# Weight loads on ScalarE's queue, paired transfers, a fourth slot and narrower tracking of overlaid tiles in a two-layer streaming encoder

## The chip, the cores and the metric

The kernel runs on the 8 cores of one Trainium2 chip (two dies of four cores). Each core works on its own stretch of a prompt and one running stream. The time is device microseconds of the slowest core, the median of several executions. Some executions fall in a slower state, in which the cores of one die or of both show a lower granted clock; they are marked slow and only fast runs are compared. PE is the matmul engine, DVE is VectorE, ACT is ScalarE, POOL is GpSimd, SP is SyncE, which here only issues transfers. PSUM is the memory, in eight banks, that matmuls write; an *evacuation* is the instruction that empties a bank.

## The reference, cut to what matters

```python
def trunk_layer(x, ...):
    xn = rms_norm(x, norm_mix)
    q, k, v, pin, gates = split(xn @ w_in)
    a  = sliding_window_attention(rms_norm(q), rms_norm(k), v, sinks)   # window 128
    pl = pool_mixer(pin)                 # trailing means over 2/4/8/16, minus the token
    g  = sigmoid(gates + gate_bias)
    x  = x + (g[0] * (a @ w_br_attn) + g[1] * (pl @ w_br_pool)) @ w_out # the mixer
    h  = causal_conv3(rms_norm(x, norm_ffn) @ w_up)
    return x + (gelu(h_gate) * h_value) @ w_down                        # the ConvFFN
# two layers; 1024 channels, 5632 up-projected channels; prompt frames and a few sampled frames
```

## The kernel before

A core works in phases: mixer of layer 1, ConvFFN of layer 1, mixer and ConvFFN of layer 2. A phase goes group by group, some 512 frames each. In a mixer group I call the gates and branch products with the next group's attention in between *stage E*, the output projection with its residual *F*, and the next projections *B*. The weights of mixer and ConvFFN do not fit together, so the tiles of one phase lie over those of the other. A small scheduler in the kernel records all operations and derives the waits. This is how it treated overlaid tiles:

```python
def op(self, eng, fn, reads=(), writes=()):
    w = list(writes)
    for r in writes:
        for x in self.over.get(r, ()):      # tiles of the other phase on the same bytes
            if x not in w:
                w.append(x)                 # counted as written too
    o.reads = tuple(reads); o.writes = tuple(w)
# _analyze: each write waits for the last writer and the readers of each name in o.writes
```

Weights and x go through SP's queue, and x tiles (`xsl`) through three rotating slots. A slot that is filled in two pieces gets the second piece only when the first has landed:

```python
def load_w(l, n):
    ...
    dma(wt[n][:, 0:sz], wb[i, :, 0:sz], [f"wb{i}"], wres(n), st)          # SP by default

def xload(src, src_res, pair, segs, zero=None):
    i = xst["n"] % NXS                                                    # NXS = 3
    for (a, b, t) in segs:
        dma(xs[i][:, :, a:b], ..., [f"xs{i}"], f"xs{i}")
```

At a change from mixer to ConvFFN ("hand-over") 17 weight tiles are loaded, the last nine after the output projection has been recorded:

```python
if nxt is None:
    load_w(l, "up6"); load_w(l, "up7")
...
stage_F(l, g)                       # issues the residual x loads
if nxt is None:
    for n in ("up8", "up9", "up10", "dn0", "dn1", "dn2", "dn3", "dn4", "dn5"):
        load_w(l, n)
```

Of the kernel before, what the change touches and what calls it, by code (L numbers as in the profile page):

```python
# [6 lines left out]
F32 = mybir.dt.float32  # L7
# [17 lines left out]
NXS = 3  # L25
NWS = 12
NFG = 9


class _Op:  # L30
    __slots__ = ("eng", "fn", "reads", "writes", "kind", "stream", "is_output", "eidx", "sidx",
                 "waits", "signal", "sig", "K", "epoch", "gidx")


class Sched:
# [24 lines left out]
    def op(self, eng, fn, reads=(), writes=()):  # L60
        o = _Op()
        w = list(writes)
        for r in writes:
            for x in self.over.get(r, ()):
                if x not in w:
                    w.append(x)
        o.eng = eng; o.fn = fn; o.reads = tuple(reads); o.writes = tuple(w)
        o.kind = "op"; o.stream = None; o.is_output = False
        o.waits = []; o.signal = False; o.sig = None; o.K = None; o.epoch = self.epoch
        o.gidx = len(self.ops)  # L70
        self.ops.append(o)
        return o

    def dma(self, eng, fn, reads=(), writes=(), stream=None, is_output=False):
        o = self.op(eng, fn, reads, writes)
        o.kind = "dma"
        o.stream = stream
        o.is_output = is_output
        if stream not in self.stream_sem:
            self.stream_sem[stream] = self.es.enter_context(self.nc.semaphore(f"dsem_{stream}"))  # L80
            self.stream_cnt[stream] = 0
        o.sidx = self.stream_cnt[stream]
        self.stream_cnt[stream] += 1
        if is_output:
            self.out_streams.add(stream)
        return o

    def _analyze(self):
# [5 lines left out]
        for op in self.ops:  # L94
# [9 lines left out]
            for wr in op.writes:  # L104
# [3 lines left out]
                for rd in readers.get(wr, ()):  # L108
                    if rd is not op and rd not in deps:
                        deps[rd] = "war"  # L110
            if op.kind == "dma":
# [3 lines left out]
                stream_last[op.stream] = op  # L115
            for r in op.reads:
# [120 lines left out]
def build_nc():  # L237
# [41 lines left out]
    with es:  # L279
# [23 lines left out]
        expAB = [sb("expA_s", [128, 8, 128], F32), sb("expB_s", [128, 8, 128], F32)]  # L303
# [4 lines left out]
        wpt = [sb(f"wpt_s{l}", [128, 512], BF16) for l in range(2)]  # L308
        kcache = [sb(f"kcache{l}", [128, 128], BF16) for l in range(2)]
        Vcache = [sb(f"Vcache{l}", [128, 2, 66], BF16) for l in range(2)]  # L310
        sph = [sb(f"sph_s{l}", [128, 4, 16], F32) for l in range(2)]
        hists = [sb(f"hists{l}", [128, NCH, 2], F32) for l in range(2)]
        Vg0 = sb("Vg0", [128, 3, 2, 66], BF16)
        Vsam = sb("Vsam", [128, 2, 66], BF16)
# [30 lines left out]
        ug = [su("f", f"ug{i}", [128, 512], F32) for i in range(3)]  # L345
        uv = [su("f", f"uv{i}", [128, 512], F32) for i in range(3)]
        for n, sz in FFN_UNITS[11:]:
            wt[n] = su("f", "w_" + n, [128, sz], BF16)

        xn1 = su("m", "xn1", [128, KT, 512], BF16)  # L350
        xn = [xn0, xn1]
        qT = su("m", "qT", [128, 4, 512], BF16, [(f"qT{j}", j * 1024, (j + 1) * 1024) for j in range(4)])
        kT = [su("m", f"kT{i}", [128, 512], BF16) for i in range(2)]
        Vw = [su("m", f"Vw{i}", [128, 4, 2, 66], BF16, [(f"Vw{i}_{t}", t * 264, (t + 1) * 264) for t in range(4)])
              for i in range(2)]
        pinb = [su("m", f"pinb{i}", [128, 528], F32) for i in range(2)]
        win = [su("m", f"win{i}", [128, 528], F32) for i in range(2)]
        dT = [su("m", f"dT{i}", [128, 4, 512], BF16, [(f"dT{i}_{j}", j * 1024, (j + 1) * 1024) for j in range(4)])
              for i in range(2)]
        P32 = [su("m", f"P32_{i}", [128, 1024], F32) for i in range(2)]  # L360
        PT = [su("m", f"PT{i}", [128, 2, 1024], BF16, [(f"PT{i}_{x}", x * 2048, (x + 1) * 2048) for x in range(2)])
              for i in range(2)]
# [3 lines left out]
        aT = [su("m", f"aT{i}", [128, 4, 512], BF16) for i in range(2)]  # L366
        tg = [[su("m", f"tg{a}{i}", [128, 512], F32) for i in range(2)] for a in range(2)]
        mixT = su("m", "mixT", [128, KT, 512], BF16, [(f"mixT{m}", m * 1024, (m + 1) * 1024) for m in range(KT)])
        sq = [su("m", f"sq{i}", [128, 512], BF16) for i in range(2)]
        srt = [su("m", f"srt{i}", [128, 512], F32) for i in range(2)]  # L370

        kg0 = su("m", "kg0", [128, HALO + TS], BF16)
        o32 = su("m", "o32", [128, 128], F32)
        kn32s = su("m", "kn32s", [128, TS], F32)
        pss = su("m", "pss", [128, 4, 16], F32)
        phist = su("m", "phist", [128, 4, 16], F32, [(f"ph{j}", j * 64, (j + 1) * 64) for j in range(4)])

        xnS = su("m", "xnS", [128, KT, 18], BF16)
        aTS = su("m", "aTS", [128, 4, 18], BF16)
        dTS = su("m", "dTS", [128, 4, 18], BF16, [(f"dTS{j}", j * 36, (j + 1) * 36) for j in range(4)])  # L380
        mixS = su("m", "mixS", [128, KT, 18], BF16, [(f"mixS{m}", m * 36, (m + 1) * 36) for m in range(KT)])

        def over(name, base, n):
            off = base[1]
            t = nc.alloc_sbuf_tensor_at(name, [128, KT, n], F32, offset=off)
            for p in range(4):
                S.region(f"{name}{p}", off + p * 8 * n, off + (p + 1) * 8 * n, "s")
            return t
        xst0 = over("xst0_", offs["P32_0"], HALO + TS)
        xst1 = over("xst1_", offs["aT0"], 512)  # L390

        actT = su("f", "actT", [128, NJ, 512], BF16, [(f"actT{j}", j * 1024, (j + 1) * 1024) for j in range(NJ)])

        corr = su("f", "corr", [128, NCH, 2], F32)
        ctmp = su("f", "ctmp", [128, NCH], F32)

        hso = su("f", "hso", [128, NCH, 2], F32)

        hpo = su("f", "hpo", [128, NCH, 2], F32)
# [28 lines left out]
        def dma(out, in_, reads, writes, stream, is_output=False, eng="sp"):  # L428
            S.dma(eng, lambda e: e.dma_start(out=out, in_=in_), reads=reads, writes=writes, stream=stream, is_output=is_output)
# [7 lines left out]
        def load_first(n):  # L437
# [4 lines left out]
            dma(wt[n][:, 0:sz], wun[i, :, 0:sz], [], wres(n), st, eng="pool")  # L442

        def load_w(l, n):
            i = l * NU + UIDX[n]
            sz = UNITS[UIDX[n]][1]
            st = f"w{wseq['n'] % NWS}"
            wseq["n"] += 1
            dma(wt[n][:, 0:sz], wb[i, :, 0:sz], [f"wb{i}"], wres(n), st)
# [13 lines left out]
        def xload(src, src_res, pair, segs, zero=None):  # L463
            i = xst["n"] % NXS
            xst["n"] += 1
            for (a, b, t) in segs:
                dma(xs[i][:, :, a:b], src[2 * pair:2 * pair + 2, :, t:t + b - a].rearrange("k p t -> p k t"),
                    src_res(pair, t, b - a), [f"xs{i}"], f"xs{i}")
# [19 lines left out]
        class NormJob:  # L488
# [12 lines left out]
            def load(self, p):  # L501
                if self.keep is not None:
                    t, nm = self.keep
                    for (a, b, c) in self.segs:
                        dma(t[:, 2 * p:2 * p + 2, a:b], self.src[2 * p:2 * p + 2, :, c:c + b - a].rearrange("k p t -> p k t"),
                            [], [f"{nm}{p}"], f"{nm}{p}")
# [46 lines left out]
            def scales(self):  # L553
                for p in range(3):
                    self.load(p)
                for p in range(3):
                    self.scale(p)
                self.load(3)
                self.scale(3)

            def stats(self):
                for p in range(4):
                    self.load(p)
                    self.stat(p)
                self.stat_end()
# [5 lines left out]
        def homes(g):  # L571
            b = g.par
            g.off = 0
            g.eX = (xn[b], f"xn{b}")
# [5 lines left out]
        def mixer_groups(l):  # L580
# [22 lines left out]
            g.att.append(dict(col=pe, n=TS, q0=0, nkc=TS, kp=(kcache[l][:, :], f"kcache{l}"), vp=(Vcache[l][:, :, :], f"Vcache{l}"),  # L603
# [5 lines left out]
            else:  # L609
                g.off = g.C0  # L610
# [45 lines left out]
        def qk_job(l, G, w, wr, c, a, gain_off, dests):  # L656
            bk = PB.get()
            X, xr = xn[G.par], f"xn{G.par}"
# [11 lines left out]

        def stage_B(l, G, fill=()):

            X, xr = xn[G.par], f"xn{G.par}"
# [15 lines left out]
            def pool_in(j):  # L689
# [3 lines left out]
                r = j % 2  # L693
                if G.own:
                    copy("pool", pinb[r][:, 0:16], phist[:, j, :], [f"ph{j}"], [f"pinb{r}"])
                    act(pinb[r][:, 16:528], psb[:, bk, 0:512], ACTF.Copy, pr(bk), [f"pinb{r}"])
                    n = 512
                else:
                    n = G.PE - G.C0
                    act(pinb[r][:, 0:16 + n], psb[:, bk, P0:G.PE], ACTF.Copy, pr(bk), [f"pinb{r}"])  # L700
                window(G, j, r, n, G.C0)
                copy("pool", phist[:, j, :], pinb[r][:, n:n + 16], [f"pinb{r}"], [f"ph{j}"])
                if G.samp is not None:
                    copy("pool", pinb[r][:, 0:16], sph[l][:, j, :], [f"sph{l}"], [f"pinb{r}"])
                    act(pinb[r][:, 16:16 + TS], psb[:, bk, G.samp:G.samp + TS], ACTF.Copy, pr(bk), [f"pinb{r}"])
                    window(G, j, r, TS, G.samp)
                    copy("pool", pss[:, j, :], pinb[r][:, 16:32], [f"pinb{r}"], ["pss"])
# [19 lines left out]
            for vi, (c, n, dst, rn, t) in enumerate(vt):  # L727
                bk = PB.get()
                for k in range(KT):
                    mm(psb[0:n, bk, 0:128], X[:, k, c:c + n], wkv[:, k, 128:256], k == 0, k == KT - 1, ["w_kv", xr], pr(bk))  # L730
                src = psb[0:n, bk, 0:128]
                copy("dve", dst, src.rearrange("p (g d) -> p g d", g=2), pr(bk), [rn])
                if t is None:
# [651 lines left out]
```

## Time and profile before

The time before is 3829.57 us (median of 3 runs; one of them, 4084.1 us, was slow; a fourth took 3828.24). I cut the profiled execution (slowest core, 3836.7 us) where the matmul stream changes its stage:

| stage, up to the first matmul named | us | PE busy |
|---|---|---|
| start, to stage E of group 1 | 259.4 | 111.5 |
| mixer 1, to stage E of the last group | 603.8 | 559.2 |
| first hand-over, to the second group's up-projection | 271.6 | 178.5 |
| ConvFFN 1, to the small group's keys in layer 2 | 882.7 | 861.4 |
| change of layer, to stage E of group 1 | 124.1 | 70.7 |
| the next group | 118.8 | 94.6 |
| mixer 2 | 513.0 | 476.7 |
| second hand-over | 239.5 | 172.9 |
| ConvFFN 2 | 823.9 | 820.1 |

Length minus PE busy is the time in which the matmul engine stood still, 491 us in all. The prediction shows these views with slightly other cuts in the hand-overs and at the change of layer.

### The profile page before, as it was taken

Reading aid. Unit: us, or ns where it says so; the run is one execution under the profiler, and the core shown is the slowest. Engines: PE = TensorE matmul, PEld = TensorE weight load, DVE = VectorE, ACT = ScalarE, POOL = GpSimd, SP = SyncE. Lnnn points to the kernel's source line nnn. Section 1 sums busy time; section 2 is a strip of 40 time slices with the busy share of each in tenths; the row PEclk is TensorE's granted clock in tenths of the full one; section 3 lists DMA queues with packets and bytes.
Section 4 is the critical chain, followed back from the end, with each engine's and each line's share of the span. In section 5 each row is a group of like instructions: output and inputs, shape, how many; then the busy total and the mean of one; then the engine's idle time right before and its main releaser. Section 6 shows DMA issues by size and latency. Waiting matters only on the chain.

```text
span 3836.7 us, 54933 instructions; the slowest of 8 cores (3823.3 to 3836.7 us)
## 1 busy us (share of the span) xinstructions
PE 3345.6 (87%) x17810; PEld 1621.7 (42%) x17810; DVE 2135.0 (56%) x3383; ACT 1545.1 (40%) x2432; POOL 1186.7 (31%) x1084
## 2 busy tenths in 40 slices
PE   1579999996599999999975879999966999999999
PEld 0344444442244444444432434444423455555554
DVE  1345455542376776666643444555426766666666
ACT  1244444431234555444433434433314444444444
POOL 1234443321123333322234333333213222333322
PEclk9789999998799999999987989999988999999999
DMA  6326666446623333333353223233252222222221
GB/s 128 69 74 132 127 130 128 122 109 165 185 79 103 92 85 90 95 98 101 106 170 92 50 82 97 88 94 104 76 192 91 81 73 80 80 79 79 79 64 40
DMA packets 186666, 384.37 MB, mean 100 GB/s; under 512 B 32880, under 2 KB 112400, under 8 KB 178384
## 3 DMA queue, kind: packets, MB, share of 16 engines
q1 hardware_dynamic: 181088, 324.00, 28.0%
q0 software_dynamic: 5296, 56.86, 9.6%
q8 instruction: 147, 2.41, 0.3%
q14 instruction: 135, 1.11, 0.1%
HBM read 368.09 MB, written 115.41 MB: 126 GB/s over the span
## 4 chain that ended last, share of the span: by engine, by line
PE 62%; DMA 17%; DVE 6%; POOL 5%; ACT 4%; issue 4%; SPq 1%; DVEq 0%; ACTq 0%; POOLq 0%
PE psb L413 61%; DMA xsl_67<-xT 3%; POOL win_114 L419 1%; DMA xsl_67<-xm 1%; POOL win_115 L419 1%; DMA xsl_66<-xT 1%; DMA xst__146<-xT 1%; DMA xsl_67<-x 1%; POOL PT_121 L419 1%; DMA xst__147<-xT 1%; DMA xsl_66<-x 1%; DMA xsl_66<-xm 1%; DMA xsl_68<-x 1%; ACT P_0_118 L416 1%; DVE xn_71 L422 1%
## 5 line engine op out<-in xcount | busy, mean ns | idle before, releaser
L419 POOL TENSOR_TENSOR actT<-ug_94,uv_97 128x480 bf16<-128x480 f32 (+3 forms) x126 | 148.7, 1180 | 1057.1 <-ACT ug_94 L416 939.6
L416 ACT ACTIVATE ug_94<-psb,pv 128x480 f32<-128x480 f32 (+3 forms) x144 | 106.4, 739 | 698.2 <-PE psb L413 520.5
L422 DVE SCALAR_TENSOR_TENSOR ug_94<-psb,pv,ug_94 128x480 f32<-128x480 f32 (+3 forms) x288 | 202.7, 704 | 137.5 <-ACT hso L416 73.5
L422 DVE SCALAR_TENSOR_TENSOR uv_97<-psb,pv,uv_97 128x480 f32<-128x480 f32 (+3 forms) x288 | 202.3, 702 | 17.2 <-issue 0.6
L422 DVE SCALAR_TENSOR_TENSOR ug_96<-psb,pv,ug_96 128x480 f32<-128x480 f32 (+3 forms) x252 | 177.6, 705 | 52.4 <-ACT ug_96 L416 27.9
L422 DVE SCALAR_TENSOR_TENSOR ug_95<-psb,pv,ug_95 128x480 f32<-128x480 f32 (+3 forms) x252 | 177.4, 704 | 22.8 <-ACT ug_95 L416 6.7
L419 POOL TENSOR_TENSOR actT<-ug_95,uv_98 128x480 bf16<-128x480 f32 (+3 forms) x126 | 148.7, 1180 | 128.9 <-ACT ug_95 L416 116.4
L422 DVE SCALAR_TENSOR_TENSOR uv_99<-psb,pv,uv_99 128x480 f32<-128x480 f32 (+3 forms) x252 | 177.0, 702 | 14.7 <-DVE uv_99 L422 0.9
L422 DVE SCALAR_TENSOR_TENSOR uv_98<-psb,pv,uv_98 128x480 f32<-128x480 f32 (+3 forms) x252 | 177.3, 704 | 14.0 <-DVE uv_98 L422 0.5
L419 POOL TENSOR_TENSOR actT<-ug_96,uv_99 128x480 bf16<-128x480 f32 (+3 forms) x108 | 127.4, 1179 | 159.3 <-ACT ug_96 L416 120.8
L413 PE MATMUL psb<-xn_71,w_up_83 128*128 128x482 bf16 (+3 forms) x576 | 122.4, 373 | 55.3 <-DVE xsl_68 L422 55.3
L419 POOL TENSOR_TENSOR win_114<-pinb_113 128x526 f32<-128x526 f32 (+7 forms) x40 | 37.1, 928 | 412.0 <-ACT pinb_113 L416 411.7
L419 POOL TENSOR_TENSOR PT_121<-P_0_118,expA_s 128x1024 bf16<-128x1024 f32 (+1 forms) x34 | 81.4, 2394 | 248.8 <-ACT P_0_118 L416 248.8
L413 PE MATMUL psb<-xn_71,w_up_86 128*128 128x482 bf16 (+3 forms) x576 | 122.7, 373 | 35.6 <-DVE ug_94 L422 35.6
L413 PE MATMUL psb<-xn_71,w_up_85 128*128 128x482 bf16 (+3 forms) x576 | 121.1, 370 | 33.0 <-DVE ug_94 L422 33.0
L416 ACT ACTIVATE P_1_119<-psb 128x1024 f32<-128x1024 f32 (+2 forms) x69 | 67.8, 983 | 198.3 <-POOL PT_120 L419 99.4
L413 PE MATMUL psb<-actT,w_dn_100 128*128 128x480 bf16 (+3 forms) x576 | 139.7, 366 | 0.8 <-DVE ug_94 L422 0.8
L413 PE MATMUL psb<-actT,w_dn_101 128*128 128x480 bf16 (+3 forms) x576 | 139.2, 365 | 0.0
L413 PE MATMUL psb<-actT,w_dn_102 128*128 128x480 bf16 (+3 forms) x576 | 138.8, 364 | 0.0
L416 ACT ACTIVATE uv_97<-psb,pv 128x480 f32<-128x480 f32 (+3 forms) x144 | 106.8, 741 | 79.2 <-PE psb L413 79.0
L413 PE MATMUL psb<-actT,w_dn_103 128*128 128x480 bf16 (+3 forms) x576 | 137.6, 362 | 0.0
L413 PE MATMUL psb<-actT,w_dn_104 128*128 128x480 bf16 (+3 forms) x576 | 137.2, 361 | 0.0
(317 smaller groups left out, 7352.0 us busy)
## 6 DMA issues: line engine op xcount, KB each, us to landing
wb<-wun POOLq DMA_DIRECT2D x42, 1024.0 KB, 9.9
xsl_68<-x SPq DMA_DIRECT2D x35, 512.0 KB, 4.1
xsl_68<-xT SPq DMA_DIRECT2D x31, 512.0 KB, 5.1
xsl_66<-x SPq DMA_DIRECT2D x31, 512.0 KB, 4.9
xsl_67<-x SPq DMA_DIRECT2D x30, 512.0 KB, 5.0
xsl_66<-xT SPq DMA_DIRECT2D x29, 512.0 KB, 5.9
xsl_67<-xT SPq DMA_DIRECT2D x28, 512.0 KB, 5.3
xm<-xsl_67 SPq DMA_DIRECT2D x27, 512.0 KB, 3.3
```

The source lines that it names most:

```text
L413: S.op("pe", lambda e: e.matmul(out=out, lhsT=lhsT, rhs=rhs, start=start, stop=stop), reads=reads, writes=writes)
L416: S.op("act", lambda e: e.activation(out=out, in_=in_, func=func, **kw), reads=reads, writes=writes)
L419: S.op(eng, lambda e: e.tensor_tensor(out=out, in0=a, in1=b, op=op), reads=reads, writes=writes)
L422: S.op("dve", lambda e: e.scalar_tensor_tensor(out=out, in0=a, scalar=s, in1=b, op0=op0, op1=op1), reads=reads, writes=writes)
```

## The change

It means to take the idle time out of the start, the hand-overs and the change of layer: weights on ScalarE's queue so that x does not stand behind them, two pieces of a slot issued together, a fourth slot, three pin buffers, a batched small group in layer 2, and overlaid tiles that are waited for but not counted as written. It also moves the *casts*, transfers on POOL's queue that turn the next weights from f32 into bf16 in memory, out of the last mixer group and the first ConvFFN group of layer 1. The core of the diff:

```diff
-NXS = 3
+NXS = 4
...
-        w = list(writes)
-        for r in writes:
-            for x in self.over.get(r, ()):
-                if x not in w:
-                    w.append(x)
-        o.eng = eng; o.fn = fn; o.reads = tuple(reads); o.writes = tuple(w)
+        o.alias = tuple(dict.fromkeys(x for r in writes for x in self.over.get(r, ())))
+        o.eng = eng; o.fn = fn; o.reads = tuple(reads); o.writes = tuple(writes)
...
+            for al in op.alias:            # wait for its last writer and its readers
+                w = last_writer.get(al)
+                if w is not None and w not in deps:
+                    deps[w] = "waw"
+                for rd in readers.get(al, ()):
+                    ...
+                c = op.chain               # pieces of one tile do not wait for each other
+                while c is not None:
+                    deps.pop(c, None)
+                    c = c.chain
...
-            dma(wt[n][:, 0:sz], wb[i, :, 0:sz], [f"wb{i}"], wres(n), st)
+                dma(wt[n][:, 0:sz], wb[i, :, 0:sz], [f"wb{i}"], wres(n), st, eng="act")
...
-        pinb = [su("m", f"pinb{i}", [128, 528], F32) for i in range(2)]
+        pinb = [su("m", f"pinb{i}", [128, 528], F32, [(f"pinb{i}h", 0, 64), (f"pinb{i}", 64, 2112)]) for i in range(3)]
...
-                stage_B(1, gs[0])
+                tables(1)
+                stage_B_small(1, gs[0])
...
-                    if m in (1, 3, 5) and i > 0:
+                    if m in (1, 3, 5) and i > 0 and nxt is not None:
                         cast_next()
...   (a new memory layout, the order of the first loads, both first norms of layer 2
...    inside the last up-projection, sums on VectorE in the start)
```

## The prediction

> **What bounds the kernel now.** I read the share line first (PE 87% busy, next DVE 56%), then busy time cut at the places where the matmul stream changes its stage, then the matmul and queue timelines inside the bad stages. The cut is this; its columns are the stretch, its length, and for each engine busy us and count, then granted clock, DMA share and GB/s:
>
> ```profile
> 0.00:259.35 259.35, 111.48 (x765) 69.30 (x766) 83.88 (x168) 68.43 (x117) 72.34 (x109) 0.84 0.46 96
> 259.35:863.15 603.80, 559.16 (x3134) 261.60 (x3132) 304.30 (x491) 244.89 (x333) 225.40 (x193) 0.99 0.55 120
> 863.15:1101.17 238.02, 145.00 (x629) 61.95 (x628) 102.58 (x168) 64.73 (x137) 48.38 (x49) 0.81 0.54 146
> 1101.17:1982.50 881.33, 881.33 (x4351) 425.94 (x4350) 598.46 (x880) 409.46 (x641) 269.82 (x224) 1.00 0.39 103
> 1982.50:2141.43 158.93, 84.25 (x526) 40.13 (x525) 56.05 (x111) 48.98 (x89) 62.16 (x88) 0.72 0.30 89
> 2141.43:2260.23 118.80, 94.61 (x722) 47.44 (x720) 50.45 (x107) 40.16 (x66) 35.22 (x31) 0.90 0.38 95
> 2260.23:2773.24 513.01, 476.72 (x2671) 222.86 (x2668) 259.69 (x419) 206.95 (x282) 181.40 (x144) 0.99 0.27 84
> 2773.24:2979.53 206.29, 139.72 (x630) 61.62 (x629) 98.84 (x168) 63.07 (x137) 44.46 (x44) 0.85 0.43 142
> 2979.53:3836.70 857.17, 853.33 (x4399) 430.90 (x4397) 580.77 (x875) 398.45 (x634) 247.48 (x202) 1.00 0.25 73
> ```
>
> Subtract PE from the length: start 148 us idle, mixer 0 45, the first hand-over from mixer to ConvFFN 93, the change of layer 75 + 24, mixer 1 36, the second hand-over 67. The two ConvFFN bodies (881 and 857 us) have no idle time at full clock: nothing in the change can move them. All 491 us of idle are in the other 2098 us, and there the clock is low too. Why, in the first hand-over, is in SP's queue (start, us held, instruction):
>
> ```profile
> 916.56 20.85 SPq L429 DMA_DIRECT2D xsl_67<-xm  x2
> ```
>
> Weights and x share one in-order queue. An x load in two pieces holds it until its first piece has landed, and each weight load waits for the one before, because both overlay the same old tile. The same coarse tracking shows in the view of waits (total, times, longest):
>
> ```profile
> ACT ug_94 L416 <- DMA w_up_93<-wb: 136.4, 2, 77.1
> ...
> POOL actT L419 <- DMA w_dn_105<-wb: 117.5, 2, 59.0
> ```
>
> The first PSUM evacuation of each ConvFFN waits for the last up weight, and the first activation tile for the last down weight: neither needs them; they only overlay a common old tile. The matmul timeline pays (the bracket is the idle time before the line):
>
> ```profile
> 62.32 1.06 PE L413 MATMUL psb<-nhl,ones_s 128*128 128x400 bf16 x2 [62.32 <-DVE nhl L426]
> ...
> 595.19 1.89 PE L413 MATMUL psb<-xn_71,w_kv 128*128 128x512 bf16 x8 [1.13 <-DVE xsl_67 L422]
> 603.02 1.89 PE L413 MATMUL psb<-xn_71,w_pin 128*128 128x512 bf16 x8 [2.27 <-DVE xsl_66 L422]
> 617.26 0.38 PE L413 MATMUL psb<-sq_133,bones_s 128*128 128x512 bf16 x1 [2.18 <-ACT sq_133 L416]
> ...
> 971.73 9.33 PE L413 MATMUL psb<-xn_71,w_up_83 128*128 128x482 bf16 x32 [36.10 <-DVE xsl_68 L422]
> 1004.28 8.43 PE L413 MATMUL psb<-xn_71,w_up_85 128*128 128x482 bf16 x32 [16.71 <-DVE ug_94 L422]
> 1033.65 5.84 PE L413 MATMUL psb<-xn_71,w_up_86 128*128 128x482 bf16 x16 [17.68 <-DVE ug_94 L422]
> ...
> 2004.45 0.59 PE L413 MATMUL psb<-nhl,ones_s 128*128 128x512 bf16 x1 [20.60 <-POOL nhl L426]
> ```
>
> The 36.10 us are residual x loads stuck in that queue. The other two waits name DVE, but DVE and ACT stood idle then: after eight half-steps all eight banks were full, and 1004.28 is just after w_up_93 landed (about 1002), as 1033.65 (w_up_86) is after w_dn_105 landed (about 1030). A unit of 32 matmuls that takes 6.67 us at full clock takes 9.33 after such a gap.
>
> **What the Trainium skill says.** "DMA: Bandwidth & Descriptors", section "Anatomy of one DMA": a semaphore wait is taken on the issuing sequencer before dispatch, so a waiting transfer blocks those behind it. The trace agrees (20.85 us held). The same page, "Issuing engines are not separate DMA queues": all queues share the 16 engines, so ScalarE's queue adds no bandwidth, only a second line to stand in. Loads one at a time took 4.8 us per MB (218 GB/s), while the DMA view of 940 to 1030 us has slices of 393 and 430 GB/s, so there is room. "TensorE: Matmul & The Clock Gate", Part 1: an idle window of about 3.4 us drops PE to half clock. The trace agrees: granted clock 0.50 from 940 to 970 us. "GPSIMD Engine Reference", opening: VectorE is roughly twice as fast elementwise; here a 128x1024 f32 add is 2.34 us on POOL and 1.23 on DVE.
>
> **The change, part by part** (lengths after, built from durations before).
>
> *Start, 259 to about 165 us.* The eight pieces of the first x tile went one by one and ended at 41 us; then hvt landed at 57.6 and held DVE. Now all are issued at once (8 x 0.4 us), the hvt copy sits on POOL, and weight loads no longer wait for each other. Estimate: x landed at 18, four squares and the adds to 24 (as from 58 to 62.7 before), root, Ln, Exp 3 us, scaling 5.8 us: first projection at 33 to 35 instead of 71; w_pin, behind hvt on POOL, may hold it to 40. Group 0's projections took 42 us with 25 idle (10.7 for one sph table that now comes early); I take 25. Group 1's take 25 (24 us of DVE, which now does windows and both mask products). Folding 4. Then group 0's stage E beside group 1's attention: 42 us before, paced at 7.1 us a step by exp, POOL product 2.35, PV; unchanged. Output 6, next projections 23. Sum 40+25+25+4+42+6+23 = 165. **-95.**
>
> *Mixer groups, 89.8 to 84.6 us each.* A fourth slot lets all four residual loads start as the scaling frees the slots, so 1.13 + 2.27 go. Three pin buffers with a separate history piece take away ACT's waits on POOL (93 us in 37 waits), so most of the 2.18 goes: 5.2 us off. Attention bubbles, some 3 us, stay. Six periods and 2.5 us at the end in mixer 0: -34; five and 2.7 in mixer 1: -28. **-62.**
>
> *Hand-overs, 238 to 144 and 206 to 143.* Weights up0 to up7 are issued during the last stage E (41.5 us) and up8 to dn5 at the end of the output projection (13.9). The evacuation no longer waits for up10 nor the activation tiles for dn5, so the 36.1, 16.7 and 17.7 go and 1.5 stays. ConvFFN group 0 then runs at once; it is bound by DVE (4 x 0.70 us and two small corrections per step): 12 steps took 46 us, so 22 take 82 to 84 rather than 71. With the first down block 4: 41.5+1.5+0.6+13.9+82+4 = 144. **-94 and -63.**
>
> *Change of layer, 159 to 91.* Both first norms are now done inside the last up-projection, so the 20.6 goes; 9 us of down matmuls remain; batched group 0 is 80 short matmuls, V and two norms, 7 us against 20 before; group 1 with no attention inside 22; the present waits of 3.3 and 9.5 us (at 2089) before group 2's normalized tile, 13; group 2 22; but five attention steps are now left over with no matmuls beside them, at 1.0 + 2.35 + about 1.4 = 4.8 us each, less an overlap: 18. **-68.** Next group, 119 to 99: the small group's two-piece loads (4.78 and 6.80 waits) are no longer chained. **-20.**
>
> Sum 95+62+94+63+68+20 = 402; 3830 - 402 = 3428. New waits that I have not found cost something; I add 12 and say **3440 us**.
>
> **Rivals.** (1) *DMA takes the place of the queue.* In a hand-over's 57 us some 8 MB of weights and 8 MB of x must move, 280 GB/s, against 210 to 227 in the serial stretches. Against it: the peaks above, and up(k) is needed only 6.5 us after up(k-1). If true, 15 us each time and 15 in the start: 3485. (2) *ACT blocks.* A weight load that waits for PE stops tanh and PSUM evacuation behind it. The listing shows only up6, up8 and up9 waiting on PE, where ACT has nothing else to do; so I give it 10%: 3470. (3) *The next gate is the norm chain* (load, square, three POOL adds of 2.35, root, scale): it ends 8 us before stage E now, so it should fit; if x loads slow down under the weights, each hand-over keeps 15 us and each mixer period 2: 3490. (4) *All of it overlaps better than I think*, above all stage E of group 0: 3380.
>
> **Range and chances.** My errors are about 20 us each in start and layer change, 15 in each hand-over, 2 us in each of 11 periods: some 40 in all, with rivals 1 and 3 pulling upward. Range 3370 to 3545. For less than 2% gain, 310 of 402 us would have to fail: faster 0.96, same 0.03, slower 0.01.
>
> **What would show it.** Right: first matmul near 25 us; E of group 1 near 165; 84 to 85 us per mixer period; no idle over 5 us before w_up matmuls; no wait of 20 us before the layer change; ConvFFN bodies unchanged within 1%. Wrong: ACT idle behind a weight DMA, PE waiting for w_eg or w_up with DMA share near 1, or a start still over 200 us.

## The result, and the profile after

The median is 3507.0 us (4 runs, 3467.38 to 3609.06), inside the stated range. But two of those four runs were slow; the fast ones took 3467.4 and 3468.9 us (a later one 3470.1). The ratio of the fast runs is 0.906 (95% interval 0.904 to 0.908). Ratios here are the mean time of one kernel's fast runs over that of the other's of the same rounds, so not quite the ratio of the medians quoted. All comparisons below use fast runs, about 3468 us, which is 28 us above the 3440 that I said.

The page of the changed kernel: share of the span for each engine, and the granted clock in 40 slices (9 is 0.9 or more).

```profile
PE 3286.3 (95%) x17807; PEld 1606.0 (46%) x17807; DVE 2247.6 (65%) x3432; ACT 1539.9 (44%) x2419; POOL 1154.2 (33%) x1020
...
PEclk8999999999999999999987999999999999999999
```

PE does the same work in 59 us less, because it rarely falls to the low clock, and idles 180 us in place of 491. The busy time cut at the instructions of the table above, in the changed kernel (stretch, length, busy us and count of PE, weight loads, DVE, ACT, POOL, then granted clock, DMA share, GB/s):

```profile
0.00:174.27 174.27, 102.00 (x765) 64.16 (x766) 99.70 (x215) 67.52 (x117) 49.24 (x65) 0.90 0.69 144
174.27:723.73 549.46, 541.67 (x3133) 258.18 (x3131) 345.96 (x496) 243.78 (x333) 222.76 (x193) 1.00 0.56 138
723.73:913.15 189.42, 172.90 (x790) 77.44 (x789) 119.38 (x204) 69.11 (x141) 45.05 (x44) 0.95 0.52 166
913.15:1773.90 860.75, 860.75 (x4244) 415.86 (x4243) 594.28 (x859) 412.79 (x644) 281.96 (x235) 1.00 0.41 115
1773.90:1883.56 109.66, 67.00 (x471) 33.30 (x470) 56.54 (x96) 40.67 (x68) 48.74 (x62) 0.73 0.24 76
1883.56:1983.41 99.85, 90.74 (x721) 46.23 (x720) 54.06 (x102) 40.22 (x66) 35.01 (x31) 0.95 0.47 113
1983.41:2451.59 468.18, 461.54 (x2670) 219.98 (x2668) 296.15 (x423) 206.50 (x282) 181.02 (x144) 1.00 0.30 99
2451.59:2641.96 190.37, 169.55 (x789) 76.23 (x788) 116.07 (x197) 67.63 (x141) 43.06 (x44) 0.96 0.51 163
2641.96:3465.80 823.84, 820.10 (x4239) 414.58 (x4237) 565.40 (x842) 391.71 (x629) 247.36 (x202) 1.00 0.22 70
```

Side by side with the prediction's own terms (the two profiles, 3836.7 and 3465.8 us):

| stage | predicted | measured |
|---|---|---|
| start | -95 | -85.1 |
| mixers 1 and 2 | -62 | -54.3 - 44.8 = -99.1 |
| hand-overs | -94 - 63 = -157 | -82.1 - 49.2 = -131.3 |
| wait before the change of layer, and the change | -68 | -21.9 - 14.4 = -36.3 |
| next group | -20 | -19.0 |
| sum | -402 | -370.8 |

So the sum is near, but only because the mixers gave 37 us more and three other stages 10, 26 and 32 us less. The profile is of the slowest core, and in the changed kernel the cores differ: its hand-overs take 179.1 to 189.4 and 171.0 to 190.4 us on the eight cores, 185.6 and 180.1 on average, so a difference of hand-overs between two slowest cores is not the whole story. Three readings show where the terms missed.

**Mixers.** In the groups of instructions (count, busy us, mean ns of one, then idle time before them and what ended it), the second exponential of each attention step stands out in the kernel before:

```profile
L416 ACT ACTIVATE P_1_119<-psb 128x1024 f32<-128x1024 f32 x65 | 66.5, 1023 | 178.5 <-POOL PT_121 L419 86.4 <-POOL PT_120 L419 80.0 <-PE psb L413 12.1
```

The same group in the changed kernel:

```profile
L426 ACT ACTIVATE P_1_106<-psb 128x1024 f32<-128x1024 f32 x65 | 66.2, 1018 | 0.0
```

ACT waited 166 us for POOL's mask product PT, which neither reads nor writes P_1. The kernel's own placement says why: P_1 (bytes 180992 to 185088) and the PT tile (from 185088) both lie under the ConvFFN tile w_dn3, so both counted as writes of w_dn3. This is the false dependency that I had found in the ConvFFN's first step, in a place where I had not looked.

**Hand-overs.** The matmul timeline of the second hand-over, changed kernel (start, us, instruction, in brackets the idle time before it):

```profile
2511.14 8.15 PE L423 MATMUL psb<-xn_60,w_up_72 128*128 128x460 bf16 x32 [3.74 <-DVE xsl_54 L432]
2524.37 5.14 PE L423 MATMUL psb<-xn_60,w_up_73 128*128 128x460 bf16 x16 [5.08 <-DVE xsl_56 L432]
```

and DVE's timeline, the residual add that it waits for:

```profile
2523.43 0.69 DVE L432 SCALAR_TENSOR_TENSOR xsl_56<-psb,xsl_56 128x512 f32<-128x512 f32 x1 [6.69 <-DMA xsl_56<-x]
```

The banks of the output projection stay full until the residual tile is there. In the kernel before, this hand-over had a wait of 19.25 us at the same place, so it has shrunk, not gone; the wait of 36.1 us in the first hand-over has become three of 2.3, 3.1 and 2.4.

**Change of layer.** POOL and DVE run beside each other there. First POOL, then DVE, in the changed kernel:

```profile
1798.05 2.36 POOL L429 TENSOR_TENSOR xsl_55<-xsl_54,xsl_55 128x1024 f32<-128x1024 f32 x1
```

```profile
1798.06 2.38 DVE L429 TENSOR_TENSOR win_117<-win_117,invc_s 128x16 f32<-128x16 f32 x1 [6.05 <-POOL win_117 L429]
```

A 128x16 product, which takes 0.17 us elsewhere on this timeline, took as long as POOL's add. Section "SBUF: two separate sides" of the Trainium skill's page "SBUF — State Buffer" says that DVE and GpSimd share a port pair under an exclusive lock, and that the later one blocks for the whole instruction; for a DVE instruction with two SBUF inputs, like this product, that holds against a GpSimd instruction that reads SBUF, like this add. The trace agrees: 2.38 us against 0.17.

### The profile page after: what moved, and what is told of

Read it like the earlier page. It is cut to its first block, busy times and chain, and to the rows that moved or that the text cites. A ratio compares the mean times of both kernels' runs of the same rounds, so it can differ in the third digit from the quotient of the medians.

```text
span 3465.8 us, 54146 instructions; the slowest of 8 cores (3429.7 to 3465.8 us)
## 1 busy us (share of the span) xinstructions
PE 3286.3 (95%) x17807; PEld 1606.0 (46%) x17807; DVE 2247.6 (65%) x3432; ACT 1539.9 (44%) x2419; POOL 1154.2 (33%) x1020
## 4 chain that ended last, share of the span: by engine, by line
PE 86%; DVE 6%; DMA 3%; issue 2%; ACT 2%; SPq 1%; POOL 1%; DVEq 0%; ACTq 0%; POOLq 0%
PE psb L423 86%; DMA xsl_57<-x 1%; DMA xst_152<-xT 1%; DMA xsl_57<-xT 1%; DVE xn_60 L432 1%; SPq L439 1%; DVE ug_85 L432 1%; DVE uv_87 L432 1%; DVE ug_83 L432 1%; DVE ug_84 L432 1%; DVE uv_86 L432 1%; DVE uv_88 L432 0%; PE psb L887 0%; DVE xn_100 L432 0%; ACT srt_128 L426 0%
## 5 line engine op out<-in xcount | busy, mean ns | idle before, releaser
L426 ACT ACTIVATE ug_83<-psb,pv 128x480 f32<-128x480 f32 (+3 forms) x144 | 106.2, 738 | 554.8 <-PE psb L423 533.5
L432 DVE SCALAR_TENSOR_TENSOR uv_86<-psb,pv,uv_86 128x480 f32<-128x480 f32 (+3 forms) x288 | 202.5, 703 | 17.7 <-DVE uv_86 L432 0.9
L432 DVE SCALAR_TENSOR_TENSOR uv_87<-psb,pv,uv_87 128x480 f32<-128x480 f32 (+3 forms) x252 | 177.3, 704 | 15.7 <-ACT uv_87 L426 0.7
L429 POOL TENSOR_TENSOR PT_108<-P_0_105,exp_131 128x1024 bf16<-128x1024 f32 (+1 forms) x33 | 75.5, 2289 | 281.8 <-ACT P_0_105 L426 267.8
L426 ACT ACTIVATE uv_86<-psb,pv 128x480 f32<-128x480 f32 (+3 forms) x144 | 106.8, 741 | 88.8 <-PE psb L423 88.8
L423 PE MATMUL psb<-xn_60,w_up_73 128*128 128x482 bf16 (+3 forms) x576 | 123.9, 375 | 12.4 <-DVE xsl_56 L432 8.2
L426 ACT ACTIVATE uv_87<-psb,pv 128x480 f32<-128x480 f32 (+3 forms) x126 | 93.4, 742 | 83.9 <-PE psb L423 83.9
L423 PE MATMUL psb<-xn_60,w_up_72 128*128 128x482 bf16 (+3 forms) x576 | 119.1, 365 | 6.1 <-DVE xsl_54 L432 3.7
L426 ACT ACTIVATE uv_88<-psb,pv 128x480 f32<-128x480 f32 (+3 forms) x126 | 93.4, 741 | 67.4 <-PE psb L423 67.3
```

The costliest lines, as they stand in the source:

```text
L423: S.op("pe", lambda e: e.matmul(out=out, lhsT=lhsT, rhs=rhs, start=start, stop=stop), reads=reads, writes=writes)
L426: S.op("act", lambda e: e.activation(out=out, in_=in_, func=func, **kw), reads=reads, writes=writes)
L429: S.op(eng, lambda e: e.tensor_tensor(out=out, in0=a, in1=b, op=op), reads=reads, writes=writes)
L432: S.op("dve", lambda e: e.scalar_tensor_tensor(out=out, in0=a, scalar=s, in1=b, op0=op0, op1=op1), reads=reads, writes=writes)
```

## The experiments

Stage lengths of the profiled execution of each kernel, in us, cut as above. The run with weights on SyncE's queue is left out; the twelfth run has the same queue. The VectorE run (e9) is left out, as its die's clock was lower in mixer 1. The runs e2, whose new layout needs the new rule, and e8, whose result is wrong, are told below only.

| kernel | start | mixer 1 | hand-over 1 | ConvFFN 1 | change | next | mixer 2 | hand-over 2 | ratio |
|---|---|---|---|---|---|---|---|---|---|
| before | 259.4 | 603.8 | 271.6 | 882.7 | 124.1 | 118.8 | 513.0 | 239.5 | 1 |
| changed | 174.3 | 549.5 | 189.4 | 860.8 | 109.7 | 99.9 | 468.2 | 190.4 | 0.906 |
| e3 pieces unpaired | 192.0 | 549.4 | 203.7 | 860.5 | 109.7 | 101.8 | 468.1 | 203.3 | 0.917 |
| e4 three slots | 173.9 | 565.7 | 207.4 | 858.1 | 108.7 | 103.3 | 472.2 | 203.3 | 0.917 |
| e5 before + rule | 255.7 | 563.0 | 230.3 | 870.4 | 119.1 | 107.9 | 480.4 | 194.3 | 0.952 |
| e6 before + queue | 257.5 | 602.8 | 251.6 | 872.0 | 123.7 | 118.6 | 518.7 | 222.5 | 0.988 |
| e7 before + both | 249.5 | 567.9 | 241.6 | 869.9 | 119.5 | 108.2 | 480.8 | 208.0 | 0.957 |
| e10 unbatched | 176.3 | 549.4 | 190.9 | 858.1 | 115.4 | 99.6 | 468.0 | 191.4 | 0.906 |
| e11 two pin buffers | 180.0 | 566.3 | 192.4 | 858.1 | 110.5 | 102.0 | 481.4 | 187.5 | 0.915 |
| e12 best | 177.6 | 549.4 | 173.7 | 858.1 | 94.3 | 100.2 | 468.1 | 168.8 | 0.891 |

### e1: the queue undone

```diff
-                dma(..., wres(n), st, eng="act")
+                dma(..., wres(n), st, eng="sp")
```

> The changed kernel with one thing undone: the layer weights are issued on SyncE's queue again, between the x loads; everything else of the change stays. Theory A (the queue itself was a main cause): weight loads that wait for PE or DVE to leave an old tile hold the x loads behind them, so each hand-over gets 15 to 25 us longer and the layer change 10 to 20: 3468 becomes 3510 to 3540. Rival B (the false dependencies were the cause, the queue only their carrier): without them a weight load rarely waits, the queue hardly stands, and the time stays within 10 us of 3468.

Measured: correct, fast runs 3433.5 and 3432.4 us, ratio 0.895 (0.893 to 0.897). It is faster than the changed kernel, so theory A fell, and so did the rival's "within 10 us". Moving the weights to ScalarE's queue costs 35 to 40 us once the rest of the change is there (fast runs differ by some 35 us; 0.906 less 0.895 is 0.011 of 3835, 42 us). It does not fall on all cores alike: in a fast run the changed kernel's cores end between 3430 and 3468 us, those of e1 between 3421 and 3432.

### e2: the old overlay rule

```diff
-        o.alias = tuple(dict.fromkeys(x for r in writes for x in self.over.get(r, ())))
-        o.writes = tuple(writes)
+        o.alias = ()
+        o.writes = tuple(dict.fromkeys(list(writes) + [x for r in writes for x in self.over.get(r, ())]))
```

> The changed kernel with the old overlay rule: a write to a tile again counts as a write of every tile that shares its bytes; weights stay on ScalarE's queue. Theory B (false dependencies): the weight loads of a hand-over go one after the other again at about 5 us per MB, the first evacuation waits for the last up weight and the first activation tile for the last down weight, 30 to 50 us for each hand-over, 10 to 20 for the layer change, 10 to 30 in the start: 3560 to 3640. Theory A (the queue): under 40 us, since x loads no longer stand behind the weights: under 3510.

Measured: correct, fast runs 3957.8 and 3959.5 us, slower than the kernel before, and far above what either theory said. Even the ConvFFN groups of layer 1 take 121 us instead of 107.6, for the change's new layout sets other tiles over each other. The run shows that the new layout cannot do without the new rule. It does not say what the rule was worth to the old kernel; for that the rule must be added to the kernel before.

### e3: pieces unpaired

```diff
-                c = dma(xs[i][:, :, a:b], ..., [f"xs{i}"], f"xs{i}", chain=c)
+                c = dma(xs[i][:, :, a:b], ..., [f"xs{i}"], f"xs{i}")
     (the same in NormJob.load and in both stores)
```

> The changed kernel in which the second piece of an x tile waits for the first again (loads and stores; the halves of the first weights stay paired). My theory of the start: the first x tile comes as eight pieces of which each waits for its predecessor, ending at 35 to 41 us instead of about 20, so the start gets 12 to 18 us longer, and the two-piece tiles of the small group and of the two ConvFFN groups with the sample cost 3 to 8 us each: 3490 to 3510. Rival: the start is held by the transfer of the weights and of the second x tile, so the later first tile is absorbed: under 8 us in all.

Measured: correct, fast runs 3513.8 and 3517.1 us, ratio 0.917 (0.915 to 0.919). The start is 17.7 us longer (14 on the average of the cores), as expected, and each hand-over 13 to 14 us (17 to 18 on average), well above the 3 to 8 that I gave its two-piece tiles. The rival fell.

### e4: three slots

```diff
-NXS = 4
+NXS = 3
     (three loads ahead in a norm, the fourth after the second sum; two residual loads ahead)
```

> The changed kernel with three x slots, used as before the change (first three tiles of a norm at once, the fourth when the second has been added in, two residual loads ahead). If the missing slot caused the waits between output projection and next projection that I gave it, the mixer period grows from 81.4 to about 84.5 us, 11 periods, and each ConvFFN hand-over by some 5 us: 3500 to 3520. Rival: the mixer period was short because the queue and the false dependencies are gone, and a slot more only buys distance: under 10 us, period under 82.2.

Measured: correct, fast runs 3516.6 to 3518.2 us, ratio 0.917 (0.916 to 0.919). The total is as my theory had it, but it comes from elsewhere: the hand-overs grow by 18.0 and 12.9 us, mixer 1 by 16.3 and mixer 2 by only 4.0. On the average of the cores the hand-overs grow by 20 and 21 us, mixer 1 by only 8.5 and mixer 2 by 4.2. The fourth slot is worth 0.7 to 2.7 us per mixer period, less than I thought, and more at the hand-overs.

### e5, e6, e7: the rule alone, the queue alone, both

e5 puts only the `alias` lines of the diff above into the kernel before, e6 only `eng="act"` in `load_w`, e7 both.

> The kernel before with one part of the change alone: overlaid tiles are tracked by their own accesses, so a write waits for the last writer and the readers of the tiles under it but does not count as a write of them. Weights stay on SyncE's queue, three slots, pieces unpaired. Theory B after the first runs (false dependencies are the main cause; the queue is not): the waits of 16.7 and 17.7 us in each hand-over, the serial weight loads there, in the start and at the layer change go, some 150 to 220 us: 3610 to 3690. Theory A (queue): under 60 us, above 3775.

> The kernel before with another part alone: weight loads on ScalarE's queue, with the old overlay rule. Theory A: x loads no longer stand behind weights that wait, so the 36 us in the first hand-over and its like in the second and at the layer change shrink: 60 to 100 us, 3735 to 3775. Theory B: the weight loads still wait for each other, and on ScalarE's queue they stop the evacuations behind them as well, so little is gained or something lost: 3810 to 3880.

> The kernel before with the overlay rule and ScalarE's queue together. From the run with weights on SyncE's queue, which beat the changed kernel by 35 to 40 us, I expect the same sign here: 10 to 40 us slower than the rule alone. If the two parts needed each other, it would be faster than the rule alone by over 20 us.

Measured, all correct: the rule alone 3646.6 and 3652.2 us, ratio 0.952 (0.950 to 0.954); the queue alone 3787.8 to 3793.0 us, ratio 0.988 (0.986 to 0.990); both 3669.3 to 3673.9 us, ratio 0.957 (0.956 to 0.959). So the rule is worth some 185 us by itself, half of the whole gain. The queue gives 47 us beside the old rule, which fits neither range that I had given (3735 to 3775 and 3810 to 3880), and takes 22 beside the new one: it was a remedy for stalls that the rule removes at the root, and where those are gone only its price is left. With the queue alone, the evacuations still stand behind weights, as theory B said. This is the view of waits of e6 (total, times, longest):

```profile
ACT ug L416 <- DMA w_dn<-wb: 109.0, 2, 55.1
```

The rule alone also settles the mixers. Stage E with its attention takes 51.3 us in most groups before, 47.7 in e5, and 47.7 in the changed kernel; the rest of a period goes from some 38 to 35.8 and 33.7. Of the gain of a period, 3.6 us are thus the false wait for PT, and no other part of the change is needed for them.

**The moved casts.** One thing stands out in these three runs and in the kernel before: the first hand-over is 26 to 36 us longer than the second on the average of the cores (before 28, e5 36, e6 26, e7 31). In the changed kernel and the fast profiles of runs built on it it is 3 to 7 us longer, and its matmul work is some 6 us more. The four kernels issue three casts in the first hand-over before its up-projection and two within it, and none in the second; the changed kernel has none in either. In the kernel before, 890 to 940 us:

```profile
wb<-wun POOLq DMA_DIRECT2D x3, 1024.0 KB, 14.9
...
xsl_67<-xm SPq DMA_DIRECT2D x1, 464.0 KB, 20.4
xsl_68<-xm SPq DMA_DIRECT2D x1, 464.0 KB, 4.1
```

The load of 20.4 us ran beside two casts and a weight tile, the load of 4.1 us after the casts had landed. So some 24 us of the first hand-over's gain are, by my estimate, those of the moved casts: on the slowest cores the rule (e5), pairs (e3) and slot (e4), less the queue (e12), sum to 58 of its 82 us, while in the second hand-over the same sum gives all of its 49. No run moves the casts alone, so this is read from the traces and not tried.

### e8: the small group's attention earlier

```diff
     (on e1)
-                stage_B(1, gs[1], js)
+                stage_B(1, gs[1], merged(att_steps(1, gs[0]), js))
-                stage_B(1, gs[2], merged(att_steps(1, gs[0]) + att_steps(1, gs[1]), ...))
+                stage_B(1, gs[2], merged(att_steps(1, gs[1]), ...))
```

> The changed kernel with weights on SyncE's queue and, in addition, the small group's attention back inside the projections of group 1 of layer 2, so that only group 1's own steps run inside group 2's. In the changed kernel four to five attention steps of 6.3 us each run with no matmuls beside them just before stage E (25 us). If those steps are late only because seven steps stand in one stage, 8 to 15 us of them go: 3418 to 3426 against 3433 for the queue alone. If DVE, POOL and ACT are what the layer change is short of, the time moves by under 4 us.

Measured: wrong result (the first exponential overwrote the raw pool map before it was scaled; the recorded order was wrong, not the waits; e12, with that order mended, is correct). The instructions are the same in number, so the time still tells something: 3427.6 to 3428.6 us, ratio 0.894. The total moved by 5 us, between what my theory and the rival said. The change of layer took 106.6 us on the average of the cores, against 109.9 in e1, so most of what the steps gave up came back as other waits, nearly as the rival said.

### e9: VectorE instead of POOL at the change of layer

```diff
     (on e1)
+                ast["eng"] = "dve"         # running sums and first mask product
                 tables(1)
                 stage_B_small(1, gs[0])
                 job = mix_norm(1, gs[2])
+                job.eng = "dve"            # the norm's adds
     (and back to "pool" before the first stage E)
```

> The changed kernel with weights on SyncE's queue and, at the layer change only, the running sums of groups 1 and 2, the adds of group 2's norm and the first mask product on VectorE instead of POOL, as the change itself does in the start. In the trace of the changed kernel a 128x16 product on DVE takes 2.4 us there instead of 0.17 while a 2.36 us add runs on POOL, and the DVE mask product 2.55 instead of about 1.1. If POOL's use of shared ports is what stretches the layer change, the attention tail's step falls from 6.3 to about 5 us and the waits for mixT go: layer change 109.7 to 94 to 101, total 3418 to 3425 against 3433. If DVE itself is the bound there, the time stays or grows: 3430 to 3440.

Measured: correct, runs 3421.8, 3422.7 and 3452.7 us (the last, the profiled one, had a lower clock on one die) and a slow one of 3646.2. The ratio, 0.896 (0.888 to 0.903), does not tell it from e1; the stretch does. The change of layer takes 98.3 to 103.5 us on the eight cores, 100.3 on average, against 108.4 to 112.7, on average 110.3, in the changed kernel and 109.9 in e1, which has the same queue as e9. Two mask products on VectorE, from its timeline in e9:

```profile
1873.43 2.35 DVE L429 TENSOR_TENSOR PT<-P,exp 128x1024 bf16<-128x1024 f32 x2
```

Both together take less than the one product did beside POOL (2.55 us), and a step of the tail falls from 6.36 to 5.26 us. POOL's work beside it is what stretched this stage, not VectorE's own work. How much of that is the port lock and how much the longer time that POOL itself takes (2.36 us for an add of 128x1024) this run does not separate.

### e10: the small group unbatched

```diff
-                stage_B_small(1, gs[0])
+                stage_B(1, gs[0])
+                copy("dve", xnS[:, :, :], xg0[:, :, gs[0].C0:gs[0].N], ["xg0"], ["xnS"])
```

> The changed kernel (weights on ScalarE's queue) with the small group of layer 2 projected by the ordinary code, one bank per product, instead of the batched one. My prediction gave the batching 13 us (20 us before, 7 after). If that is right, the layer change grows from 109.7 to about 122 us and the total from 3468 to 3478 to 3484. If the windows and DVE's order set the pace there anyway, under 5 us.

Measured: correct, fast runs 3473.7 and 3474.4 us, ratio 0.906 (0.904 to 0.909): not told apart from the changed kernel by the total. The stretch itself is 115.4 against 109.7 us on the slowest cores, 115.1 against 110.3 on the average of eight. Batching gives 5 us, not 13.

### e11: two pin buffers

```diff
-        pinb = [... [(f"pinb{i}h", 0, 64), (f"pinb{i}", 64, 2112)]) for i in range(3)]
+        pinb = [... [(f"pinb{i}", 0, 2112)]) for i in range(2)]
     (history copied before the evacuation again)
```

> The changed kernel with two pin buffers whose history is part of the same tracked tile, as before. My prediction put the wait of 2.18 us before the block sums in each mixer period down to them. If right, the mixer period grows from 81.4 to 83 to 84 us, 11 to 12 periods: 3485 to 3500. If the false dependencies or the slots were what delayed ScalarE, the period stays under 82 and the total under 3475.

Measured: correct, all four runs fast, 3503.6 to 3515.1 us, ratio 0.915 (0.912 to 0.918). The mixer period grows from 81.4 to between 82.8 and 85.0 us, and the wait that I had named is back in the view of waits of e11:

```profile
ACT pinb L426 <- POOL pinb L436: 64.6, 28, 3.6
```

My theory holds: the mixers grow by 16.8 and 13.2 us, 2.3 to 2.8 us for each period where I had 2.18.

### e12: the best version found

```diff
     (on e9)
+                stage_B(1, gs[1], merged(js, [[]] + att_steps(1, gs[0])))
     (and the small group's differences after its key and value tiles)
```

> The run before (weights on SyncE's queue, VectorE's sums, adds and mask products at the layer change, 3422 in its fast runs) with two changes of order: the small group's attention starts one step into the projections of group 1, after the mapped pool weights have been made (the earlier try overwrote them and gave a wrong result), and the small group's differences are emitted after its key and value tiles, so that VectorE scales the keys first. If the tail of attention steps and the wait for the keys are what is left of the layer change, it falls from 102.3 to 88 to 95 us: total 3409 to 3416. If the steps only move into waits of the same size inside group 1, as in the earlier try: within 3 us of 3422. The ConvFFN bodies and hand-overs (about 174 and 169 us) should not move.

Measured: correct, fast runs 3414.8 to 3418.8 us, ratio 0.891 (0.889 to 0.893), the fastest kernel. The change of layer falls to 94.3 us on the slowest core, 94.8 on average, at the upper end of what I expected. It also gives a fast profile of the hand-overs with weights on SyncE's queue. Transfers in the second hand-over (KB each, median us to landing), changed kernel:

```profile
xsl_54<-x SPq DMA_DIRECT2D x1, 512.0 KB, 11.5
...
xsl_57<-x SPq DMA_DIRECT2D x1, 512.0 KB, 26.5
```

and e12:

```profile
xsl<-x SPq DMA_DIRECT2D x4, 512.0 KB, 6.4
```

with this matmul timeline in e12, where nothing comes between output projection and up-projection:

```profile
2476.89 23.46 PE L423 MATMUL psb<-xn,w_up 128*128 128x460 bf16 x120
```

Section "Queues, rings and completion order" of the skill's page "DMA: Bandwidth & Descriptors" says that a DMA engine goes round-robin between the queues that have work for it, and takes one queue's descriptors in order. The traces agree: with two queues, the four residual tiles, issued at 2498 to 2504 us, shared the engines with weight tiles of which the first, w_up_78, was not needed before 2561 us, and landed after 11.5 to 26.5 us; in one queue they stood ahead of the weights and landed after 6.1 to 7.1. How they shared is in the view of queues of the changed kernel, 2515 to 2535 us (packets, MB, share of the engines), where q10 carries weights and q1 x:

```profile
q10 hardware_dynamic: 785, 5.69, 74.8%
q1 hardware_dynamic: 784, 1.52, 24.2%
```

The packets are equal in number, one for one, but those of x are about a quarter as long, so x got a fifth of the bytes. The hand-overs are 15.7 and 21.5 us shorter on the slowest cores, 11.8 and 9.5 on the average of eight; two cores of the changed kernel did the second one in 171 us, as fast as e12. The order in one queue acts as a priority.

## Why the prediction was right or wrong

**Outcome.** The median lies in the range, and so do the fast runs, 3468 us. That the total came within 28 us is partly luck: the steps below miss by 10 to 37 us and in both directions, and a part of the first hand-over's gain comes from casts that the prediction did not know of.

**Right: false dependencies at the hand-overs.** The waits of 16.7 and 17.7 us are gone, and the rule alone takes 41 and 45 us from the two hand-overs (e5). The ConvFFN bodies did not move, the wait of 20.6 us before the change of layer went (-21.9), and the next group came out at 99.9 for 99.

**Wrong: "Attention bubbles, some 3 us, stay."** The mixer period fell to 81.4 us, not 84.6. The rule alone removes 3.6 us from stage E (e5), as ACT no longer waits for POOL's product. The line was on the page before: P_1 waiting for PT, a tile that it does not share. I had put the 7.1 us step of group 0 in the start down to the same pace and left it "unchanged"; there stage E went from 42.2 to 34.7 us, and to 35.0 with the rule alone. The rest was of the right kind: pin buffers 2.3 to 2.8 us per period (e11) for 2.18, and the slot 0.7 to 2.7 (e4) for 3.4.

**Wrong: "the 36.1, 16.7 and 17.7 go and 1.5 stays."** Waits of 2.3, 3.1 and 2.4 us stayed of the 36.1 in the first hand-over, and 10.6 us in place of 19.25 in the second, since ScalarE's queue does not only set x free from the weights, it also sets weights against x. The 36.1 itself I had read as x stuck behind weights, and the 20.85 us held as the price of pieces; but two casts and a weight tile were in flight beside that load, and by the estimate above their going is some 24 us of the 82. The third rival had both the size (15 us kept in each hand-over; measured 12 and 14) and the cause: "if x loads slow down under the weights". I held it for unlikely because the peaks of the DMA view left room; but for a tile that is needed first it is the order that counts. The section of the Trainium skill that I cited, "Issuing engines are not separate DMA queues", also says that the transfers of different engines interleave with each other; I had taken from it only that there is no gain in bandwidth, not that x would take turns with weights. That moving the weights was a gain at all is the largest error in the reasoning: it is one only beside the old rule (e6), and a loss of 22 (e7) to 40 us (e1) beside the new one.

**Wrong in size: the start.** The first projection came at 35.6 us, close to the 33 to 35 of the estimate and 4.4 before the 40 of the sum. But the projections of groups 0 and 1 took 32.8 and 37 us for 25 each, 20 us more, and the shorter stage E (7.3 us) made up for only a part of it. The first matmuls of the changed kernel:

```profile
26.91 1.06 PE L423 MATMUL psb<-nhl,ones_s 128*128 128x400 bf16 x2 [26.91 <-DVE nhl L436]
35.57 2.83 PE L423 MATMUL psb<-xn_60,w_kv 128*128 128x400 bf16 x8 [7.61 <-DVE wpt_133 L1149]
```

and the busy time of its first 85 us, columns as before:

```profile
0.00:85.00 85.00, 31.18 (x172) 17.30 (x173) 42.74 (x103) 24.72 (x48) 15.56 (x37) 0.86 1.00 187
```

The DMA engines are busy all the time, at 187 GB/s. The last piece of group 1's x tile lands at 50.7 us, and its norm holds PE for 10 us. This is my first rival, in the start alone. No run here took transfers out of the start, so that they bind is read from the trace and not tried.

**Wrong in size: the change of layer.** It lost 14.4 us beside the 21.9, where I had 47. The batched group gives 5 us, not 13 (e10). The tail of attention steps takes 25 us and not 18, 6.36 us a step and not 4.8, and group 1 was slower than its matmuls, both where POOL works beside DVE: moving POOL's work away gives 10 us on the average of the cores (e9), and the order of e12 another 5.5. My term for a step used POOL's 2.35 us and forgot that DVE's product, which takes 1.2 us alone, took 2.55 beside it. In the mixers the same happens (the product takes 1.23 us before and 2.52 after; that the false wait had kept the two engines apart is my reading, no run tests it), but there PE sets the pace and it costs nothing.

**Small slips of the prediction.** The second ConvFFN body does have 3.8 us of idle (857.17 less 853.33), so 487 and not 491 us lie in the other stages; the "4.8 us per MB" of loads one at a time holds for the down tiles, while up tiles took 5.6 to 5.9; and the start's own sum gives -94, not -95.

**Still open.** With weights on SyncE's queue and the last order, some 30 us of idle remain at the change of layer, of which 8.8 are group 2's scaling on DVE before its first matmul; I did not try to split that wait.

## What to carry to other kernels

When memory is overlaid, a write must wait for what lies under it but must not count as a write of it, or unrelated tiles get ordered through an old tile that nobody uses; look for waits between two instructions that share no data, in every stage and not only where the stall is largest. Do not move transfers to a second queue before such waits are gone: one queue in the order of need is a priority, two queues took turns here packet by packet, and the one with the shorter packets got the fewer bytes. Ask also what else is in flight beside a load that is waited for, such as bulk casts for a later stage. Where DVE sets the pace, count POOL's instructions beside it as DVE's time. And compare a stage on all cores before its length on the slowest one is given a cause.

## What the Trainium skill lacked or had wrong

- "DMA: Bandwidth & Descriptors": the rules say that spreading transfers over several issuing engines does not help; they do not say that it can cost. Here 512 KB loads landed after 11.5 to 26.5 us with weights on a second queue and 6.4 us with all on one, and each hand-over was 15.7 to 21.5 us longer on the slowest core, 9.5 to 11.8 on average; with packets of unequal length, turns one for one (785 and 784) gave 5.69 MB to one queue and 1.52 to the other.
- "TensorE: Matmul & The Clock Gate", Part 1: the page says that dense matmuls on three cores of a die bring its clock to 13/16 for as long as the load lasts. The value is seen here, its reach and its lasting are not: in e1's slow profile cores 2 and 3 ran mixer 1 and ConvFFN 1 at 0.81 and 0.82 and then mixer 2 and ConvFFN 2 at 1.00, while core 0 of the same die ran mixer 1 at 1.00 and mixer 2 and ConvFFN 2 at 0.81. In fast runs all eight cores ran the ConvFFN bodies at 0.99 to 1.00.
- No page treats dependency tracking over overlaid tiles; the rule alone moved the time from 3836 to 3650 us.
